# A hybrid decoder layer on one core: the gated linear units ahead of the first two heads' chains, the convolution beside them

## The chip, the core and the metric

The kernel runs on one core of a Trainium2 chip, as one launch. The metric is the device time in microseconds (us). The core has a matrix engine (PE), a vector engine (DVE), an engine for activations and copies (ACT), a general engine (POOL) and an engine that issues DMAs (SP). Each works through its own list of instructions in order and waits for the others by semaphores; the transfers run on DMA queues.

## The reference

One layer for 512 prompt tokens and 8 samples of 8 tokens, 576 columns in all. Shortened:

```
x  = x + 0.5 * swiglu(rmsnorm(x))                       # ffn1, 1024 -> 2816 -> 1024
z  = rmsnorm(x) @ w_in                                  # inputs of all branches and three gates
y_a = rwkv7(z)        # 8 heads of 64: s = s*w + (s@-kk)*kka + v*k per token, o = s@r;
                      # then group norm, + bonus, * g, @ w_rwkv_out
u   = z[:256] * sigmoid(z[256:512])                     # gated linear unit (GLU)
y_b = silu(layernorm(depthwise_conv31(u))) @ w_conv_out # convolution of 31 taps
y_c = cross_attention(z, 256 memory tokens) @ w_xattn_out
m   = sum(sigmoid(gate_n) * y_n for n in a, b, c) @ w_o # merge
x   = x + m
x   = x + 0.5 * swiglu(rmsnorm(x)); y = rmsnorm(x)     # ffn2
```

The new states of the heads, of the token shift and of the convolution are returned too.

## The kernel before

All activations lie with channels on the 128 partitions and the 576 tokens along the free dimension, in two halves of 288 columns. A product in full precision is made of three products of parts: `split` (L94 to L96) rounds an operand to a high part (ACT, L95) and subtracts it for a low part (DVE, L96); L109 multiplies high by high, high by low, low by high. So a projection of 128 rows over 1024 inputs is 48 products of 288 columns on L109, and it needs `wh` from ACT and `wl` from DVE.

The program is ffn1, then the middle, then the merge and ffn2. The middle is written out as a list of steps, `PLAN` (L28), and the instructions of every engine get their place by a scheduler that walks through the program in this order and lets later work in where an earlier one would wait. The steps are:

- A0: the cross-attention, whose result is `oc`.
- P0 to P3, `prep`: the four pairs of heads (128 channels each). Each makes three projections (144 products), the decay factors (a reciprocal, L888), the keys' norm (L137, L147), factors `ra`, `kb`, and the masked products of these, `gr` (PE L945, DVE L947). The last L947 of a pair ends its part that the inverse needs.
- I0 to I3, `inverse`: a triangular inverse by elimination on DVE. A DMA takes the blocks out of `gr` and back into `lt` (L1031, L1033, on SP), then come L1034 to L1049, and DMAs bring the result back.
- J0 to J3, `joined`: 32 small products of PE for it (L1067, L1075), with a copy on ACT between (L1070).
- B0 and B2, `chains`: for two pairs, eight chunks of 64 tokens one after another, each with small products (L1122, L1132, L1139), copies (L1137, L1140), the product for the state (L1143) and the new state on DVE (L1165); then the sample's chunk and `mixed` for both pairs, with the group norm (L984, L137, L147) and DVE's L990, L992, L994, L997.
- G0, `glu`: four projections, 192 products, for the convolution's input.
- C0, `conv`: on DVE, 60 taps of 512 columns (L730) and 60 of 64 columns (L731) with L727 at the start of each half, then the layer norm over channels (PE L127, L137, L147).
- Y, X, Z with a count: the gates of the three branches, eight of each, which nothing before the merge waits for. A Y block is one projection (48 products) and a store; X (after the attention) and Z (after the convolution, whose result is split to `cb0h`) are a projection and 12 products more, a multiplication on DVE (L858), a sum with what is stored already (L862) and a store.
- L0, `load_ya`, and then the merge.

The gates are the work that fills PE while DVE does the inverses and the chains. Step P1's function stands under the same name as P2's, so a line tells the kind of work and not its pair.

Ahead of ffn1, `busy` (L209) gives PE a number of products of zeros while the first inputs are loaded (POOL's memset, L224, releases them). `low_rank`, at the start of the middle, makes decay, learning rate and gate of the heads in products of 288 columns; the gates' eviction from PSUM is L691.

Of the kernel before, what the change touches and what calls it, by code (L numbers as in the profile page):

```python
# [9 lines left out]
ALU = mybir.AluOpType  # L10
# [14 lines left out]
NORMED = 1  # L25

ROOMS = (8, 9, 10, 11, 12, 0, 1, 2, 3, 4, 8, 9, 10, 11, 5, 6, 7, 0, 8, 9, 10, 11)
PLAN = ("A0 P0 I0 Y3 G0 P1 J0 I1 Y3 X1 J1 B0 X3 P2 I2 Y2 X2 P3 J2 X2 I3 C0 Z2 J3 B2 Z4 L0 Z2")  # L28
PADN = 8 * 65 + 8 * 9
GRP = 11  # L30
NPROB = 36
# [18 lines left out]
class _Builder:  # L50
# [122 lines left out]
    def build(self):  # L173
        tc, a = self.tc, self.a
        with ExitStack() as st:
# [22 lines left out]
            with ExitStack() as sf:  # L198
                F = sf.enter_context
                self.psum(F, p=8)  # L200
                x1p = F(tc.tile_pool(name="x1", bufs=1))
                fp = F(tc.tile_pool(name="f1", bufs=2))
                hp = F(tc.tile_pool(name="h1", bufs=1))
                self.strassen_pools(F)
                self.weight_pools(F, 2, 1)
                x = [x1p.tile([128, N], F32, name=f"x{k}") for k in range(8)]
                idle = fp.tile([128, H], F32, name="m1")[:, :128]
                self.G.memset(idle, 0.0)
                self.busy(idle, idle, 16)  # L209
                self.dma(x[0][:, :H], a["x"][:, 0, :H])  # L210
                self.dma(self.pv, a["pv"])
                raw = []
                for k in range(4):
                    w = self.wtile()
                    raw += [w[:, 384 * k:384 * (k + 1)] for k in range(2)]
                for k in range(8):
                    if k:
                        self.dma(x[k], a["x"][:, k, :])
                    self.dma(raw[k].rearrange("p (j c) -> p j c", j=3),
                             a["wu1"][:3, :, 128 * k:128 * (k + 1)].rearrange("j p c -> p j c"))  # L220
                    if not k:
                        self.dma(x[0][:, H:], a["x"][:, 0, H:])
                self.dma(self.cst, a["cst"])
                self.G.memset(self.eps[:, 0:1], 64e-5)  # L224
                self.G.memset(self.eps[:, 1:2], 1e-5)
                self.A.activation(self.eps[:, 0:1], self.eps[:, 0:1], AF.Copy)
                c = _COLS["mu"]
                self.V.tensor_scalar(self.omu, self.pv[:, c:c + 15], -1.0, 1.0, ALU.mult, ALU.add)
                c = _COLS["ka"]
                self.V.tensor_scalar(self.oka, self.pv[:, c:c + 4], -1.0, 1.0, ALU.mult, ALU.add)  # L230
                self.ffn(x, hp, fp, "g1", a["wu1"], a["wd1"], self.mix_norm, raw, lambda: self.mem_load(mp),
                         (self.mem_k, self.mem_v))
# [18 lines left out]
                    "Z": [(lambda i=i: self.gated(gp, 1, "cb", self.cb, i, 0)) for i in range(8)]}  # L251
            for step in PLAN.split():
                n = int(step[1:])
# [377 lines left out]
    def low_rank(self, zp):  # L631

        V, A, T, a, b1 = self.V, self.A, self.T, self.a, self.b1
        two = lambda name, n: zp.tile([128, 2, n], F32R, name=name)
        sub = lambda o, x, hi: V.tensor_tensor(o, x, hi.bitcast(F32), ALU.subtract)
        wh, wl, gh, gl = two("wh", 512), zp.tile([128, 512], F32R, name="wl"), two("gh", 512), zp.tile(
            [128, 512], F32R, name="gl")
        xs, lg, gs = two("xs", N), two("lg", N), zp.tile([128, N], F32R, name="gs")  # L640
        x = b1.tile([128, N], F32, name="k")
        self.shifted(12, x, b1)
        A.activation(x[:64], x[:64], AF.Tanh)
        for i in range(2):
            o, q = slice(64 * i, 64 * i + 64), slice(64 - 64 * i, 128 - 64 * i)
            A.copy(xs[o, i], x[o])
            sub(xs[q, i], x[o], xs[o, i])
        x = b1.tile([128, N], F32, name="r")
        self.shifted(13, x, b1)
        A.activation(x, x, AF.Sigmoid)  # L650
        self.split(lg[:, 0], lg[:, 1], x)
        x = b1.tile([128, N], F32, name="av")[:96]
        self.shifted(14, x, b1)
        A.activation(x, x, AF.Sigmoid)
        A.copy(gs[:96], x)
        sub(gs[32:64], x[32:64], gs[32:64])

        t = b1.tile([128, 1024], F32, name="lt")
        self.dma(t, a["wda"])
        t = t.rearrange("p (i c) -> p i c", i=2)  # L660
        A.copy(wh, t)
        for i in range(2):
            o = slice(64 * i, 64 * i + 64)
            sub(wl[o], t[o, i], wh[o, i])
        t = [b1.tile([128, PADN], F32, name=n)[:, :512] for n in ("w", "g")]
        for i in range(2):
            self.dma(t[i], a["wg"][:, 512 * i:512 * i + 512])
            A.copy(gh[:, i], t[i])
        sub(gl, t[0], gh[:, 0])
        sub(gh[64:96, 1], t[1][64:96], gh[64:96, 1])  # L670

        def products(*ops):
            for h in range(2):
                c = slice(h * H, (h + 1) * H)
                p = self.bank("g")[:, :H]
                for q, (l, r) in enumerate(ops):
                    T.matmul(p, l, r[:, c], start=q == 0, stop=q == len(ops) - 1)  # L677
                yield c, p

        for j in range(4):  # L680
            ch = slice(128 * j, 128 * j + 128)
            for i, (par, out, name) in enumerate((("w0", self.d_w, "bv"), ("a0", self.d_a, ("k", "r")[j % 2]))):
                t = b1.tile([128, N], F32, name=name, bufs=2 - i)
                o = slice(64 * i, 64 * i + 64)
                for c, p in products((wh[:, i, ch], xs[:, i]), (wl[o, ch], xs[o, i])):
                    A.activation(t[:, c], p, AF.Sigmoid, bias=self.par(par, j))
                self.store(out[j], t)
            t = b1.tile([128, N], F32, name=("av", "zt")[j % 2])
            for c, p in products((gh[:, 0, ch], lg[:, 0]), (gh[:, 0, ch], lg[:, 1]), (gl[:, ch], lg[:, 0]),
                                 (gh[:96, 1, ch], gs[:96])):  # L690
                A.copy(t[:, c], p)  # L691
            self.store(self.d_gt[j], t)


# [670 lines left out]
```

## Time and profile before

| | us |
|---|---|
| timed, three runs: median (lowest, highest) | 1507.62 (1499.61, 1508.52) |
| profiled execution, its own time | 1491.07 |
| its span | 1489.2 |
| PE, DVE, ACT busy | 1449.4, 1028.1, 664.4 |
| granted clock of PE, mean | 0.974 |
| middle stage, first rows of A0 to the merge | about 445 to 1001 |

Busy shares are of the span. In the table of stretches that follows in the prediction, an engine's busy time is given with its count of records, and PEclk is the share of its full clock that PE was granted.

### The profile page before, as it was taken

The page shows a single profiled execution, that of the slowest core. Times are in us where ns is not written, and L with a number is a line of the kernel's source. Part 1 is how long each engine was busy: PE and PEld are TensorE (multiplying, and loading weights), DVE is VectorE, ACT ScalarE, POOL GpSimd, SP SyncE. Part 2 cuts the span into 40 slices and gives each one's busy share as a digit, 9 for nine tenths or more (in the row PEclk, how much of TensorE's full clock was granted, in tenths as well). Part 3 has the DMA queues.
Part 4 walks back from the last instruction along what each step waited for, and adds up shares of the span by engine and source line. Part 5 has one row for each costly group of instructions (what it writes and reads, how often), then busy time and mean ns, then how long its engine had stood idle before and what let it go on. Part 6 is the DMA issues. An engine that isn't in the chain of part 4 may idle for free.

```text
span 1489.2 us, 27301 instructions
## 1 busy us (share of the span) xinstructions
PE 1449.4 (97%) x10884; PEld 1384.6 (93%) x10884; DVE 1028.1 (69%) x2059; ACT 664.4 (45%) x1348; POOL 5.0 (0%) x22
## 2 busy tenths in 40 slices
PE   9999999999999999999999887999999999999998
PEld 9999999999988889899889786889999999999997
DVE  7976777777875629896347763348578767777775
ACT  7443444444577733534355422344444433444442
POOL 0000000000000000000000000000000000000000
PEclk9999999999999999999999877989999999999999
DMA  6222222323644143344122332227322322233221
GB/s 209 72 86 86 86 85 86 98 88 99 198 149 154 57 140 80 89 124 117 49 89 88 92 114 75 74 87 258 101 85 72 94 78 86 89 89 107 85 86 64
DMA packets 98444, 151.28 MB, mean 102 GB/s; under 512 B 43997, under 2 KB 53725, under 8 KB 98317
## 3 DMA queue, kind: packets, MB, share of 16 engines
q1 hardware_dynamic: 97740, 148.95, 32.2%
q8 instruction: 85, 1.39, 0.4%
q10 hardware_dynamic: 576, 0.59, 0.1%
q14 instruction: 43, 0.34, 0.1%
HBM read 130.03 MB, written 19.48 MB: 100 GB/s over the span
## 4 chain that ended last, share of the span: by engine, by line
PE 90%; DVE 6%; issue 1%; ACT 1%; DMA 1%; SPq 0%; DVEq 0%; POOL 0%; ACTq 0%; POOLq 0%
PE p L109 50%; PE p L384 26%; DVE pr L1045 2%; DVE tt L1047 1%; PE g L945 1%; DVE wl L96 1%; PE g L677 1%; PE c L1122 1%; PE g L1153 1%; PE c L1139 1%; PE g L137 1%; DVE cc L730 1%; PE c L1086 1%; PE g L147 1%; PE c L1132 1%
## 5 line engine op out<-in xcount | busy, mean ns | idle before, releaser
L109 PE MATMUL p<-x,wh 128*128 128x288 f32 x3136 | 653.7, 301 | 4.2 <-ACT wh L95 3.5
L109 PEld LDWEIGHTS p<-x,wh 128*128 128x128 f32 x3136 | 511.8, 191 | 12.4 <-ACT wh L95 4.2
L109 PE MATMUL p<-x,wl 128*128 128x288 f32 x1568 | 472.0, 302 | 6.8 <-DVE wl L96 6.7
L95 ACT CAST wh<-w 128x512 fp32r<-128x512 f32 (+1 forms) x354 | 210.3, 600 | 260.9 <-PE p L384 100.0
L109 PEld LDWEIGHTS p<-x,wl 128*128 128x128 f32 x1568 | 298.5, 191 | 12.9 <-DVE wl L96 8.7
L96 DVE TENSOR_TENSOR wl<-w,wh 128x512 fp32r<-128x512 f32 (+1 forms) x354 | 232.5, 662 | 109.8 <-ACT wh L95 99.5
L384 PE MATMUL p<-t,wh 128*128 128x288 f32 x1088 | 224.3, 299 | 0.0
L384 PEld LDWEIGHTS p<-t,wh 128*128 128x128 f32 x1088 | 173.9, 188 | 6.4 <-DVE t L395 6.4
L384 PE MATMUL p<-b,wh 128*128 128x288 f32 x816 | 169.7, 295 | 0.0
L384 PE MATMUL p<-t,wl 128*128 128x288 f32 x544 | 160.6, 295 | 0.0
L95 ACT CAST wh<-p 128x512 fp32r<-128x512 f32 x136 | 84.5, 621 | 155.9 <-PE p L109 117.4
L384 PEld LDWEIGHTS p<-b,wh 128*128 128x128 f32 x816 | 132.8, 188 | 0.0
L96 DVE TENSOR_TENSOR wl<-p,wh 128x512 fp32r<-128x512 f32 x136 | 93.6, 688 | 50.6 <-ACT wh L95 47.8
L384 PE MATMUL p<-b,wl 128*128 128x288 f32 x408 | 120.4, 295 | 0.0
L384 PEld LDWEIGHTS p<-t,wl 128*128 128x128 f32 x544 | 102.5, 188 | 0.0
L384 PEld LDWEIGHTS p<-b,wl 128*128 128x128 f32 x408 | 76.8, 188 | 0.0
L462 DVE SCALAR_TENSOR_TENSOR x<-p,x 128x288 f32<-128x288 f32 x128 | 57.8, 451 | 21.2 <-PE p L109 21.2
L95 ACT CAST x<-t 128x576 fp32r<-128x576 f32 (+1 forms) x60 | 36.5, 610 | 44.8 <-DVE t L466 42.2
L374 DVE TENSOR_TENSOR p<-w 128x512 f32<-128x512 f32 x68 | 46.7, 686 | 2.4 <-DMA w<-wu 2.0
L374 DVE TENSOR_TENSOR p<-p,w 128x512 f32<-128x512 f32 x68 | 46.4, 682 | 0.1
L851 ACT ACTIVATE gate<-p 128x288 f32<-128x288 f32 x48 | 19.7, 410 | 55.9 <-PE p L109 50.6
L1165 DVE SCALAR_TENSOR_TENSOR st<-c,gc,mg 64x64 f32<-64x64 f32 x56 | 15.8, 283 | 41.3 <-PE c L1143 28.9
(380 smaller groups left out, 1990.9 us busy)
## 6 DMA issues: line engine op xcount, KB each, us to landing
w<-wu SPq DMA_DIRECT2D x85, 512.0 KB
w<-win SPq DMA_DIRECT2D x44, 512.0 KB
w<-wd SPq DMA_DIRECT2D x64, 256.0 KB
w<-wd SPq DMA_DIRECT2D x16, 384.0 KB
d_mb<-gate SPq DMA_DIRECT2D x16, 288.0 KB
w<-wo SPq DMA_DIRECT2D x8, 512.0 KB
d_x<-x SPq DMA_DIRECT2D x16, 144.0 KB
d_g<-gate SPq DMA_DIRECT2D x8, 288.0 KB
```

The lines of the kernel that those rows point to most:

```text
L95: self.A.copy(hi, x)
L96: self.V.tensor_tensor(lo, x, hi.bitcast(F32), ALU.subtract)
L109: self.T.matmul(p, l, x[r][:, c], start=k == 0 and i == 0, stop=k == n - 1 and i == 2)
L137: self.T.matmul(p[:, i * w:(i + 1) * w], t[:, o:o + 128], sel, start=q == 0, stop=q == len(ops) - 1)
L147: self.T.matmul(p[:, o + f - d.start:o + 128 - d.start], r[f:, i], self.con("ident")[f:, f:], start=True, stop=True)
L374: V.tensor_tensor(s, u, v, ALU.add)
L384: self.T.matmul(p, hl[l][:, c], xs[k][b][:, o], start=first and k == 0 and q == 0, stop=k == 3 and q == 2, skip_group_check=True)
L462: V.scalar_tensor_tensor(x[m][:, c], p, 0.5, x[m][:, c], ALU.mult, ALU.add)
L677: T.matmul(p, l, r[:, c], start=q == 0, stop=q == len(ops) - 1)
L851: self.A.activation(g[:, c], p, AF.Sigmoid)
L1045: V.tensor_tensor(pr, tt[:, :n, :e].unsqueeze(2).broadcast_to([np_, n, m, e]), l3[:, t:e, :e].unsqueeze(1).broadcast_to([np_, n, m, e]), A ...
L1165: V.scalar_tensor_tensor(mn[s, i, s], p, g[s], mg[s, s], ALU.mult, ALU.add)
```

## The change

The list of steps is written anew, the lead has ten empty products in place of 16, and one eviction of `low_rank` goes from ACT to DVE:

```
-PLAN = ("A0 P0 I0 Y3 G0 P1 J0 I1 Y3 X1 J1 B0 X3 P2 I2 Y2 X2 P3 J2 X2 I3 C0 Z2 J3 B2 Z4 L0 Z2")
+PLAN = "A0 P0 I0 Y2 P1 J0 Y3 I1 Y3 X2 J1 X1 G0 B0 C0 P2 I2 X3 P3 J2 X2 Z1 I3 Z2 J3 B2 Z5 L0"
...
-                self.busy(idle, idle, 16)
+                self.busy(idle, idle, 10)
...
             for c, p in products((gh[:, 0, ch], lg[:, 0]), (gh[:, 0, ch], lg[:, 1]), (gl[:, ch], lg[:, 0]),
                                  (gh[:96, 1, ch], gs[:96])):
-                A.copy(t[:, c], p)
+                V.tensor_scalar(t[:, c], p, 1.0, None, ALU.mult)
```

So G0 goes from behind the first Y blocks to the place directly ahead of B0, and C0 from behind I3 to behind B0; all eight Y blocks stand ahead of the first chains.

The first place to look at is PE's list at the end of the first chains, where the mixing (L984, L137, L147) ends. Before (`oc` is the attention's result, so the L109 rows are products of an X block):

```order
L984 MATMUL g<-ra,cst 128x320
L984 MATMUL c<-ra,cst 128x256
L137 MATMUL c<-cst,u_8234 128x2 x2
L984 MATMUL g<-ra,cst 128x256
L109 MATMUL p<-oc1h,wh 128x288
L109 MATMUL p<-oc1l,wh 128x288
L109 MATMUL p<-oc1h,wl 128x288
L109 MATMUL p<-oc0h,wh 128x288
L137 MATMUL c<-cst,u_8234 128x2 x3
L109 MATMUL p<-oc0l,wh 128x288
```

And now (`cc` is the convolution's result, `x` the normed input):

```order
L984 MATMUL g<-ra,cst 128x320
L984 MATMUL c<-ra,cst 128x256
L137 MATMUL c<-cst,u_8528 128x2 x2
L984 MATMUL g<-ra,cst 128x256
L137 MATMUL c<-cst,u_8528 128x2 x3
L147 MATMUL c<-cst,u_8547 128x128 x4
L147 MATMUL c<-cst,u_8547 128x64
L137 MATMUL g<-cst,u_8564 128x2 x5
L147 MATMUL g<-cst,u_8583 128x128 x4
L147 MATMUL g<-cst,u_8583 128x64
L127 MATMUL g<-cc_7900,cst 128x288 x2
L109 MATMUL p<-x_4949,wl 128x288
```

The products of gates and projections between the steps of the mixing are gone from there; directly behind the mixing stand the convolution's first statistic and a product of P2 with a low part of its weight.

The second place is DVE's list at the same point, behind the L992 of the second pair. Before:

```order
L992 TENSOR_TENSOR u_8271<-u_8271,g 128x512
L992 TENSOR_TENSOR u_8271<-u_8271,g 128x64
L96 TENSOR_TENSOR wl<-w,wh 128x512
L858 TENSOR_TENSOR gate<-p,gate 128x288
L994 TENSOR_TENSOR u_8271<-u_8271,bv 128x576
L858 TENSOR_TENSOR gate<-p,gate 128x288
L997 TENSOR_TENSOR u_8271<-gt,u_8271 128x576
L911 TENSOR_SCALAR rt<-rt 128x10
```

And now, the first rows of a longer piece:

```order
L992 TENSOR_TENSOR u_8565<-u_8565,g 128x512
L992 TENSOR_TENSOR u_8565<-u_8565,g 128x64
L730 SCALAR_TENSOR_TENSOR cc_7900<-up_7902,pv,cc_7900 128x512
L730 SCALAR_TENSOR_TENSOR cc_7901<-up_8034,pv,cc_7901 128x512
L994 TENSOR_TENSOR u_8565<-u_8565,bv 128x576
L730 SCALAR_TENSOR_TENSOR cc_7901<-up_8034,pv,cc_7901 128x512
L731 SCALAR_TENSOR_TENSOR cc_7901<-ue_8035,pv,cc_7901 128x64
L997 TENSOR_TENSOR u_8565<-gt,u_8565 128x576
```

Then come seven more pairs of an L730 and an L731, and then the last rows up to the first L96:

```order
L730 SCALAR_TENSOR_TENSOR cc_7901<-up_8034,pv,cc_7901 128x512
L604 SCALAR_TENSOR_TENSOR k<-z_5305,omu,zt 128x512
L730 SCALAR_TENSOR_TENSOR cc_7901<-up_8034,pv,cc_7901 128x512
L605 SCALAR_TENSOR_TENSOR k<-z_5305,omu,zt 128x64
L730 SCALAR_TENSOR_TENSOR cc_7901<-up_8034,pv,cc_7901 128x512
L96 TENSOR_TENSOR wl<-w,wh 128x512
```

So the first weight split behind L992, which came next before, now has 13 L730 and 8 L731 ahead of it; it is the one that the P2 product of the PE piece reads. Nine L730 more come behind it, between splits.

The third place is DVE's list ahead of inverse 3, whose first instruction is the L1034. Before, the last of the convolution's products (L746) and the splits of its result stand there:

```order
L746 TENSOR_TENSOR cc_6823<-cc_6823,g 128x64
L746 TENSOR_TENSOR cc_6824<-cc_6824,g 128x64
L96 TENSOR_TENSOR wl<-w,wh 128x512 x2
L96 TENSOR_TENSOR cb0l<-cc_6823,cb0h 128x576
L96 TENSOR_TENSOR cb1l<-cc_6824,cb1h 128x576
L858 TENSOR_TENSOR gate<-p,gate 128x288 x2
L96 TENSOR_TENSOR wl<-w,wh 128x256
L862 TENSOR_TENSOR gate<-gate,gm 128x576
L858 TENSOR_TENSOR gate<-p,gate 128x288 x2
L1034 MEMSET lt 108x32
```

And now, behind pair 3's last masks:

```order
L947 TENSOR_TENSOR gr<-g,cst 128x128 x2
L858 TENSOR_TENSOR gate<-p,gate 128x288 x2
L96 TENSOR_TENSOR wl<-w,wh 128x512 x2
L96 TENSOR_TENSOR wl<-w,wh 128x256
L96 TENSOR_TENSOR wl<-w,wh 128x512 x2
L858 TENSOR_TENSOR gate<-p,gate 128x288 x2
L96 TENSOR_TENSOR wl<-w,wh 128x256
L96 TENSOR_TENSOR wl<-w,wh 128x512 x2
L858 TENSOR_TENSOR gate<-p,gate 128x288 x2
L862 TENSOR_TENSOR gate<-gate,gm 128x576
L1034 MEMSET lt 108x32
```

The convolution is gone from this piece, and three gates' multiplications (L858) with the splits of their weights stand between the last masks and the inverse; the last pair is that of the Z block which the list of steps has ahead of I3.

## The prediction

> **What bounds the kernel now.** I read the page's shares first, then a table of stretches, then PE's waits.
>
> ```profile
> span 1489.2 us, 27301 instructions
> ...
> PE 1449.4 (97%) x10884; PEld 1384.6 (93%) x10884; DVE 1028.1 (69%) x2059; ACT 664.4 (45%) x1348; POOL 5.0 (0%) x22
> ...
> PEclk9999999999999999999999877989999999999999
> ```
>
> PE is the bound. The time that another order can win is what PE loses: its idle time and its low clock, and the clock row shows that the low clock lies in slices 23 to 27 of 40, some 820 to 1010 us. So I cut the middle at the points where PE goes from one plan step to the next (columns: stretch, its length, busy time of each engine with its count of records, granted clock, DMA).
>
> ```profile
> core 0: us, PE busy (x) PEld busy (x) DVE busy (x) ACT busy (x) POOL busy (x), PEclk, DMA share, GB/s
> 559.00:607.00 48.00, 45.20 (x305) 43.83 (x304) 44.72 (x95) 17.68 (x39) 0.00 (x0) 0.90 0.34 92
> 706.90:801.60 94.70, 94.30 (x788) 81.00 (x788) 47.02 (x100) 41.67 (x110) 0.00 (x0) 0.98 0.24 73
> 801.60:869.10 67.50, 60.29 (x402) 56.60 (x400) 44.60 (x110) 31.84 (x58) 0.00 (x0) 0.90 0.36 100
> 869.10:912.50 43.40, 29.71 (x246) 28.52 (x245) 29.39 (x73) 9.36 (x21) 0.00 (x0) 0.85 0.34 96
> 912.50:1001.10 88.60, 85.73 (x701) 71.94 (x701) 33.92 (x76) 35.83 (x94) 0.00 (x0) 0.84 0.24 69
> 1050.00:1075.00 25.00, 25.00 (x191) 25.00 (x190) 15.15 (x24) 10.18 (x16) 0.00 (x0) 1.00 0.28 95
> 900.00:925.00 25.00, 16.44 (x157) 15.19 (x158) 5.98 (x13) 5.67 (x14) 0.00 (x0) 0.70 0.38 97
> ```
>
> The stretch from 1050 is PE at its best: 25.00 / 191 = **0.131 us for a product** of 288 columns. The five stretches of the argument are: S1, the start to the first state product of the first chains (706.9); S2, from there to the last mask of pair 2 (801.6); S3, to J2 (869.1); S4, J2 to J3 (912.5); S5, J3 to the merge (1001.1). S1 and S2 are dense; S3 and S4 have 7.2 and 13.7 us without PE.
>
> ```profile
> PE p L109 <- DVE wl L96: 6.7, 5, 3.2
> PE c L1067 <- DMA aux<-s: 6.1, 1, 6.1
> PE p L109 <- ACT cb0h L95: 5.4, 1, 5.4
> ```
>
> These waits (from 400 to 1010 us) are for the convolution's result cb0h, for weight splits that stand behind the convolution on DVE, and for inverse 3. A wait costs twice, for the clock of 900 to 925 is 0.70 after the 6.1 us before J3.
>
> **S1.** The new plan lists, ahead of the first chains, eight Y blocks (before: six, and 54 products of the next two), the GLU, P1, and three X blocks (before four), and no P2 (before its 144 projection products). That is 42 - 60 - 144 = -162 products, and 162 x 0.131 = -21.3. Of the loss in 559 to 607 (2.8 idle and a tenth of the clock, 7 in all), where DVE was full at 44.72 of 48.00 beside the GLU, I take back 4.5 of 7, as G0 no longer stands there. Against this J1 now comes too early for inverse 1. What lies between a pair's last mask and its join:
>
> ```profile
> 801.76 1.88 SPq L1031 DMA_DIRECT2D s<-gr  x2
> 815.16 0.09 DVE L1034 MEMSET lt<- 108x32 f32 x1
> 852.01 0.53 DVE L1047 TENSOR_REDUCE tt<-pr 108x11 f32<-108x352 f32 x1
> 869.69 0.09 DVE L1034 MEMSET lt<- 108x32 f32 x1
> 900.96 0.51 DVE L1047 TENSOR_REDUCE tt<-pr 108x11 f32<-108x352 f32 x1
> 869.08 1.19 PE L1067 MATMUL c<-aux,gr 32*32 32x32 f32 x32
> 912.49 1.91 PE L1067 MATMUL c<-aux,gr 32*32 32x32 f32 x32 [6.09 <-DMA aux<-s]
> ```
>
> For pair 2 the way from the mask's store to the first elimination step took 815.16 - 801.76 = 13.4. For pair 3 the elimination took 901.47 - 869.69 = 31.8 and the way back 912.49 - 901.47 = 11.0. Inverse 1 has fewer foreign instructions between its steps than inverse 3, so I take 27, and 4.5 for its load behind a gate's store on SP: 13.4 + 27 + 11.0 + 4.5 = 56. PE has 335 products and some small ones for it, 48.5. So J1 waits 7.5 (bounds 0 and 12.3, by 31.8 in place of 27). S1 = -21.3 - 4.5 + 7.5 = **-18** (bounds -26 and -13).
>
> **S2.** Here the 48 of the 60 long convolution taps that the list of DVE places behind the first state update come in. Of the timeline of before (start, length), the ends of the parts of S2, two vector instructions of it, and the convolution's statistics on PE:
>
> ```profile
> 706.90 0.45 PE L1143 MATMUL c<-vu,kbt 128*64 128x64 f32 x8
> 774.83 0.43 PE L147 MATMUL g<-cst,u 64*128 64x64 f32 x2
> 776.22 1.17 PE L137 MATMUL g<-cst,u 128*128 128x2 f32 x10
> 801.36 0.29 DVE L947 TENSOR_TENSOR gr<-g,cst 128x128 f32<-128x128 f32 x1
> 776.69 0.76 DVE L994 TENSOR_TENSOR u<-u,bv 128x576 f32<-128x576 f32 x1
> 803.92 0.28 DVE L605 SCALAR_TENSOR_TENSOR r<-z,omu,zt 128x64 f32<-128x64 f32 x1
> 834.37 2.10 PE L127 MATMUL g<-cc,cst 128*128 128x288 f32 x8
> 849.01 1.41 PE L147 MATMUL g<-cst,rt 128*128 128x128 f32 x10
> ```
>
> The convolution's taps, all of them in one group each (busy us, mean ns):
>
> ```profile
> L730 DVE SCALAR_TENSOR_TENSOR cc<-up,pv,cc 128x512 f32<-128x512 f32 x60 | 43.3, 743 | 0.0
> L731 DVE SCALAR_TENSOR_TENSOR cc<-ue,pv,cc 128x64 f32<-128x64 f32 x60 | 14.3, 279 | 0.2
> ```
>
> And PE's products of L109 alone (PE, PEld) beside the chains:
>
> ```profile
> 707.00:775.30 68.30, 27.93 (x157) 21.96 (x158) 0.98 0.21 62
> ```
>
> The chains took 775.26 - 706.90 = 68.4, with 157 products of fill beside them. Now the fill is 54 products of P2, and none in the last four chunks and in the mixing behind them. If every product that goes shortens the chains they take 68.4 - 103 x 0.131 = 54.9; if the chains bind themselves, 68.4. PE was busy 94.30 of 94.70, so the nearer end is the lower: I take a third of the way, **59.5**. Then PE stands. P2's next product reads a weight's low half (L96), and the list of DVE has 13 L730, 8 L731, L994, L997, L604 and L605 ahead of it: 13 x 0.72 (43.3 / 60) + 8 x 0.24 (14.3 / 60) + 2 x 0.76 + 0.76 (L604, taken as L994) + 0.28 + 0.7 (L96, estimated by L994 too) = 14.5 from the end of the last L992, which is over about when PE is. Behind the product that waits, all of PE's list waits: P2's projections, the statistics, masks and X blocks. With a little of the 14.5 done beside the mixing I take **13** (bounds 0, if DVE is that far by then, and 15). Behind it are 87 products, 11.4, with the convolution's statistics among them; in S3 before, these took 849.01 - 834.37 = 14.6 with fill beside them, and DVE's last nine taps (6.5, with splits between them) end behind the first 50 products (6.6), so that the second of the statistics may wait. I take 11.4 + 7.6 = **19** (bounds 12 and 26). From pair 2's own L137 to its last mask took 801.65 - 776.22 = 25.4; I take **28**, since the stores and splits queued from the wait must be worked off first (bounds 25.4 and 31). Sum 59.5 + 13 + 19 + 28 = 119.5 against 94.7: **+25** (bounds -2 and +46).
>
> **S3.** The convolution leaves the stretch, and pair 3's projections and X blocks stay beside inverse 2, at 13.4 + 37.3 (852.54 - 815.16, the elimination with what stands between) + 11.0 + 5 for a load behind a store = 66.7 for 67.5, and the last part of P3 stands behind inverse 2 on DVE (its mask work on PE waits for L928 there, some 2 us). I take **+1** (bounds -8 and +6).
>
> **S4.** Inverse 3's first step stands on DVE behind Z's multiplication (L858), whose products follow J2 on PE: 97 products (37 of X, 60 of Z), 12.7, and their small waits and the store ahead of the load on SP, 6.3. 19 + 31.8 + 11.0 = 62 against 43.4: **+18.6**. Without that PE's own work would set it: 379 products x 0.131 = 49.6 and 5 of J2 and masks, 54.7, or +11.3, and that is the lower bound; the upper is +24, with 5 for a clock as after the wait before J3.
>
> **S5** has 48 products fewer beside the chains: **-6.3** (0 to -13, as the clock there was 0.84 and may be nearer to 1). Merge to end is the same list.
>
> **The lead and the evictions.**
>
> ```profile
> 0.99 5.95 PE L170 MATMUL p<-m 128*128 128x128 f32 x32 [0.99 <-POOL eps L224]
> 6.70 5.54 PE L109 MATMUL p<-x,t 128*128 128x288 f32 x40
> ```
>
> ```profile
> L691 ACT COPY zt<-g 128x288 f32<-128x288 f32 x4 | 1.6, 395 | 0.2
> L858 DVE TENSOR_TENSOR gate<-p,gate 128x288 f32<-128x288 f32 x32 | 14.6, 455 | 20.6 <-ACT gate L851 10.4 <-PE p L109 9.6 <-ACT vu L1140 0.6
> ```
>
> The 16 empty products leave 32 records, 5.95 / 32 = 0.186 each, so ten (20 records) end near 4.7. The first real product could start about 5.0 instead of 6.70: -1.7 (bounds -1.9, and +1.7 if its operands come no sooner and run at a lower clock). The Trainium skill ("TensorE: Matmul & The Clock Gate", Part 1, on the warm-up) says that the clock doubles after a window of about 3.4 us of busy time which runs free of the kernel's start, and counts no products; by it 3.7 us of empty products may end inside a window, real products then run at half clock for up to another 3.4 us, and this term is 0 in place of -1.7 (an estimate), the sum +20.3. No run here shows a lead of 3.7 us; behind the 5.95 of this one, 40 real products took 5.54, 0.139 each, nearly the full pace.
>
> Eight evictions of 288 columns go from ACT (0.395) to DVE, 3.2 less there and, by L858 of the same size, 8 x 0.455 = 3.6 more here. They lie under the wide projections of the attention's stretch, before 559 us; the work that hides them is PE's, so 0 (bounds -1.6 and +3.6).
>
> **Sum:** -18 + 25 + 1 + 18.6 - 6.3 - 1.7 = **+18.6**. The profiled execution took 1491.07, its span 1489.2, and would take 1509.7; the timed runs' median is 1507.62, 16.6 above it, so the forecast is 1526.
>
> **Rivals.**
>
> *The convolution fits into the chains' gaps (faster, about 1486, 0.22).* DVE was busy 47.02 of S2's 94.70; the 48 long and 8 short taps make 34.7 + 1.9, so 83.6: there is room. If DVE is through with them when the mixing ends, S2 = 54.9 + 0 + 11.4 + 2 + 25.4 = 93.7, -1; inverse 1 with 1 us of wait gives S1 -24.8, S4 +11.3. The sum is -24.8 - 1 + 1 + 11.3 - 6.3 - 1.7 = -21.5. The point is S2 below about 100: from there on the whole is faster by over 1%. Against it: PE has no fill in the last four chunks, so the chains' end is early and DVE has less time, not 94.7.
>
> *It cancels (within 1%, about 1511, 0.28).* Half of the wait, 6.5, and inverse 3 not held up, S4 +12: S2 then 110, and the sum -18 + 15 + 1 + 12 - 6.3 - 1.7 = +2, or +4 with J1 waiting 2 more. It speaks for it that each of my waits can only be smaller if PE is late.
>
> *The clock falls as well (slower, about 1545, 0.04).* Three new waits of 7 to 13 us (J1, P2, J3) each bring what 900 to 925 shows, 0.30 of 25 = 7.5 us. 18.6 + 2.5 x 7.5 = +37. The Trainium skill ("TensorE: Matmul & The Clock Gate", Part 1, the two states) says that an idle window of about 3.4 us halves the clock and a busy one of that length restores it; by it, an estimate, each wait costs 1.7 more, 5 in all, and the sum would be +24. The row shows more, as 25 us were held at 0.70.
>
> The forecast with +12 to +28 has 0.46.
>
> **Chances and range.** 1% (15 us) is about what a measurement of this kernel can tell from none. Faster by over 1%: 0.22; within: 0.28; slower: 0.50. The forecast's own range is 1519 to 1536. For 8 in 10 the range goes down to 1484, through the cancelling case and to the middle of the fast one, and up to 1548, with the upper part of S2's bounds and most of the slow clock.
>
> **What would show it.** In the changed kernel: PE waits for J1 about 7 us at the join's L1067; a wait of about 13 on DVE wl L96 after the last L147 of the first chains; L730 rows between L1165 rows; the last mask of pair 2 about 120 after the first L1143; inverse 3's L1034 19 us after J2 and a wait of about 7 before J3; no wait for cb0h. I am wrong if DVE has the taps done by the mixing's end, or if the chains with less fill take 68 again and the wait vanishes in that.

## The result, and the profile after

The changed kernel took **1522.24 us** (median of four runs, 1517.52 to 1526.69), the kernel before 1506.66 (four runs, 1499.61 to 1508.52). The ratio is 1.0112, with a 95% interval of 1.0062 to 1.0161, so 15.6 us slower; the forecast was 1526, or 18 us. In a later comparison of the same two kernels the ratio was 1.0168 (1.0095 to 1.0240). The page of the changed kernel's profiled execution, the lines that answer to those of before:

```profile
span 1515.7 us, 27281 instructions
...
PE 1465.2 (97%) x10872; PEld 1398.6 (92%) x10872; DVE 1038.8 (69%) x2067; ACT 657.7 (43%) x1337; POOL 5.0 (0%) x22
...
PEclk9999999999999999999579899799999999999999
```

The span is 26.5 us longer than that of before (1489.2). It is more than the 15.6 of the medians, since the profiled execution of before, 1491.07, lay below all of its first four timed runs, while that of the changed kernel is its fastest. The shares of the engines say nothing of it; the clock row does: its lowest digits, a 5 and a 7, now stand in slices 20 and 21, at 720 to 796, where before stood nines; another 7 stands in slice 26, in the second chains.

The stretches, cut at the same steps (the first state product, pair 2's last mask, J2, J3, the merge), and ahead of them the one from 559 on:

```profile
core 0: us, PE busy (x) PEld busy (x) DVE busy (x) ACT busy (x) POOL busy (x), PEclk, DMA share, GB/s
559.00:607.00 48.00, 45.61 (x363) 42.76 (x363) 30.63 (x57) 24.93 (x57) 0.00 (x0) 0.93 0.38 97
685.80:817.60 131.80, 111.26 (x789) 94.37 (x789) 87.54 (x170) 49.59 (x123) 0.00 (x0) 0.79 0.17 45
720.00:757.50 37.50, 31.46 (x174) 25.81 (x174) 20.40 (x38) 11.64 (x33) 0.00 (x0) 0.59 0.09 19
817.60:883.30 65.70, 60.96 (x400) 56.48 (x399) 41.38 (x101) 25.55 (x55) 0.00 (x0) 0.87 0.29 78
883.30:940.00 56.70, 54.48 (x451) 53.40 (x450) 36.39 (x87) 17.20 (x38) 0.00 (x0) 1.00 0.49 146
940.00:1024.00 84.00, 78.42 (x652) 65.20 (x652) 34.68 (x76) 34.45 (x91) 0.00 (x0) 0.85 0.31 91
1024.00:1515.70 491.70, 483.65 (x3594) 479.72 (x3594) 351.24 (x652) 197.69 (x352) 0.00 (x0) 0.99 0.31 97
```

| | before | changed | difference | forecast |
|---|---|---|---|---|
| S1 with the lead | 706.9 | 685.8 | -21.1 | -19.7 |
| S2 | 94.7 | 131.8 | +37.1 | +25 |
| S3 | 67.5 | 65.7 | -1.8 | +1 |
| S4 | 43.4 | 56.7 | +13.3 | +18.6 |
| S5 | 88.6 | 84.0 | -4.6 | -6.3 |
| merge to end | 488.1 | 491.7 | +3.6 | 0 |

S2 is the whole of the loss and more. Its row says what is wrong in it: 20.5 us without PE, and a clock of 0.79. S4 is the opposite, 54.48 of 56.70 busy at a clock of 1.00, where before had 13.7 idle. The waits of PE that ended last on DVE or on a DMA, from 440 to 1030 (total, times, longest):

```profile
PE p L109 <- DVE wl L96: 16.5, 5, 10.0
PE g L127 <- DVE k L928: 3.9, 1, 3.9
PE c L1067 <- DMA aux<-s: 0.8, 1, 0.8
```

The 10.0 is the wait behind the first chains. In the timeline of PE (start, length, then idle time ahead and what ended it) it stands right behind the mixing:

```profile
754.81 2.69 PE L147 MATMUL g<-cst,u 128*128 128x128 f32 x10 [1.73 <-ACT u L154]
758.57 2.26 PE L127 MATMUL g<-cc,cst 128*128 128x288 f32 x4 [1.07 <-DVE cc L730]
770.79 0.61 PE L109 MATMUL p<-x,wl 128*128 128x288 f32 x1 [9.96 <-DVE wl L96]
```

And in that of DVE the split that ends it comes behind the last of the taps that the list has ahead of it:

```profile
769.40 0.74 DVE L730 SCALAR_TENSOR_TENSOR cc<-up,pv,cc 128x512 f32<-128x512 f32 x1
770.06 0.68 DVE L96 TENSOR_TENSOR wl<-w,wh 128x512 fp32r<-128x512 f32 x1
```

### The profile page after: what moved, and what is told of

It is laid out like the page before. It is cut to its first block, busy times and chain, and to the rows that moved or that the text cites. A ratio compares the mean times of both kernels' runs of the same rounds, so it can differ in the third digit from the quotient of the medians.

```text
span 1515.7 us, 27281 instructions
## 1 busy us (share of the span) xinstructions
PE 1465.2 (97%) x10872; PEld 1398.6 (92%) x10872; DVE 1038.8 (69%) x2067; ACT 657.7 (43%) x1337; POOL 5.0 (0%) x22
## 5 line engine op out<-in xcount | busy, mean ns | idle before, releaser
L109 PE MATMUL p<-x,wh 128*128 128x288 f32 x3136 | 651.5, 300 | 3.1 <-ACT wh L95 1.2
L109 PEld LDWEIGHTS p<-x,wh 128*128 128x128 f32 x3136 | 511.2, 190 | 11.8 <-issue 3.4
L109 PE MATMUL p<-x,wl 128*128 128x288 f32 x1568 | 470.7, 301 | 14.9 <-DVE wl L96 14.6
L96 DVE TENSOR_TENSOR wl<-w,wh 128x512 fp32r<-128x512 f32 (+1 forms) x354 | 232.2, 662 | 147.7 <-ACT wh L95 136.7
L109 PEld LDWEIGHTS p<-x,wl 128*128 128x128 f32 x1568 | 297.8, 190 | 21.7 <-DVE wl L96 17.1
L95 ACT CAST wh<-p 128x512 fp32r<-128x512 f32 x136 | 84.5, 621 | 156.4 <-PE p L109 117.3
L96 DVE TENSOR_TENSOR wl<-p,wh 128x512 fp32r<-128x512 f32 x136 | 93.6, 688 | 51.1 <-ACT wh L95 48.2
L374 DVE TENSOR_TENSOR p<-w 128x512 f32<-128x512 f32 x68 | 46.6, 686 | 2.2 <-DMA w<-wu 1.6
L1045 DVE TENSOR_TENSOR pr<-tt,lt 108x6 f32<-108x6 f32 (+9 forms) x80 | 42.4, 530 | 1.9
L730 DVE SCALAR_TENSOR_TENSOR cc<-up,pv,cc 128x512 f32<-128x512 f32 x60 | 43.3, 743 | 0.4
```

The costliest lines, as they stand in the source:

```text
L95: self.A.copy(hi, x)
L96: self.V.tensor_tensor(lo, x, hi.bitcast(F32), ALU.subtract)
L109: self.T.matmul(p, l, x[r][:, c], start=k == 0 and i == 0, stop=k == n - 1 and i == 2)
L374: V.tensor_tensor(s, u, v, ALU.add)
L730: V.scalar_tensor_tensor(c[:, :SEQ], up[:, k:k + SEQ], w, c[:, :SEQ], ALU.mult, ALU.add)
L1045: V.tensor_tensor(pr, tt[:, :n, :e].unsqueeze(2).broadcast_to([np_, n, m, e]), l3[:, t:e, :e].unsqueeze(1).broadcast_to([np_, n, m, e]), A ...
```

## The experiments

Two theories were on trial at first. The one: the taps that now stand ahead of pair 2's weight splits on DVE cost the time, as they hold P2 and so leave PE without fill. The other: the gates and projections, moved as such, cost it. From the third experiment on the clock was the question, and then the GLU's place. The chains below are the stretch from the first state product to the end of the last L147 of their mixing.

**1. The small parts alone.** The list of steps of before, with the rest of the change.

```
-PLAN = "A0 P0 I0 Y2 P1 J0 Y3 I1 Y3 X2 J1 X1 G0 B0 C0 P2 I2 X3 P3 J2 X2 Z1 I3 Z2 J3 B2 Z5 L0"
+PLAN = ("A0 P0 I0 Y3 G0 P1 J0 I1 Y3 X1 J1 B0 X3 P2 I2 Y2 X2 P3 J2 X2 I3 C0 Z2 J3 B2 Z4 L0 Z2")
```

> The list of steps of before, with the ten empty products and the evictions of L691 on DVE. Theory (the loss is the new list's, the small parts hide or gain): the first real product starts at 5.3 instead of 6.7, the evictions show nowhere, so -1.4 and, within what can be measured, no change to before (0.99 to 1.005). Rival (the evictions on DVE, 3.6 us, or a lead too short for the clock cost time): +2 to +5, a lower clock in the first 25 us, and the merge later than 1001 by that.

Measured: 0.9965 of before (0.9919 to 1.0012). As expected; the loss is the list's.

**2. X3 ahead of the convolution.**

```
-... G0 B0 C0 P2 I2 X3 P3 ...
+... G0 B0 X3 C0 P2 I2 P3 ...
```

> The changed kernel with X3 ahead of the convolution in the list (G0 B0 X3 C0 P2 I2 P3). Theory (the first chains ran at half clock and 71.7 long because PE had no fill in their second half): the fill is back, the granted clock in the chains is 0.95 or more, they take 66 to 70, the 10 us wait for the weight split is gone, and S2 (131.8) becomes about 120 though it holds 180 products (23.6 us) more; S3 then lacks these and stays at 64 to 68 by inverse 2, with over 15 us of idle PE. In all about -10, a span of 1500 to 1511. Rival (the taps between the state updates on DVE slow the chains, with fill or without): chains of 72 or more, S2 140 or more, a span of 1520 or more.

Measured: 1.0094 (1.0061 to 1.0126), a span of 1520.8. Its S2, cut where the mixing ends:

```profile
691.30:768.30 77.00, 76.20 (x622) 63.42 (x621) 43.58 (x92) 32.36 (x86) 0.00 (x0) 0.91 0.24 65
768.30:833.90 65.60, 55.01 (x367) 50.62 (x367) 51.42 (x94) 30.26 (x65) 0.00 (x0) 0.90 0.19 62
```

The clock of the chains is higher (0.91 for 0.78), with the fill, but S2 is 142.6: P2 still stands behind the taps, and a wait of 6.8 us for its weight split is left. The total was a miss: fill alone gives nothing back, if P2 comes no sooner. All three numbers of the rival came true (chains of 77.0, S2 of 142.6, a span of 1520.8), but its reason doesn't follow from that: in experiments 7 and 8 the chains took 78.9 without a tap beside them and 78.7 with 31 long ones.

**3. The convolution behind P2.**

```
-... G0 B0 C0 P2 I2 X3 P3 ...
+... G0 B0 P2 C0 I2 X3 P3 ...
```

> The changed kernel with the convolution one step later in the list (G0 B0 P2 C0 I2 X3 P3). Theory (where the taps stand against pair 2's weight splits sets the loss, and not the GLU and gates ahead of the chains): pair 2's products become the chains' fill, their clock is 0.95 or more, pair 2's last mask comes 95 to 108 after the first state product instead of 131.8, and S3 stays within 62 to 72; in all -20 to -30, a span of 1486 to 1496, which is before or a little better. Rival (S2 is long because the gates no longer stand beside the chains, wherever the taps are): S2 120 or more, or what S2 wins S3 loses (80 or more) since the taps then hold inverse 2; a span of 1508 or more.

Measured: 1.0096 (1.0044 to 1.0147), a span of 1517.7. Pair 2's last mask came 99.4 after the first state product, and S3 took 67.3, both as expected; the clock of 0.95 was not, since P2's products fill only the first part of S2 (the first row below is the rest of it, at 0.58). The 32 us were given back later all the same:

```profile
744.60:786.50 41.90, 27.96 (x133) 23.94 (x129) 34.13 (x68) 13.12 (x30) 0.00 (x0) 0.58 0.17 51
853.80:920.90 67.10, 65.55 (x530) 62.48 (x529) 42.02 (x98) 21.81 (x48) 0.00 (x0) 1.00 0.44 128
920.90:975.00 54.10, 53.00 (x395) 43.86 (x394) 16.39 (x39) 15.45 (x48) 0.00 (x0) 0.65 0.22 65
975.00:1026.90 51.90, 47.65 (x321) 40.21 (x319) 20.25 (x43) 22.29 (x50) 0.00 (x0) 0.80 0.23 67
```

S4 (the second row) is now 67.1 long and full of gates' products, which is more than inverse 3 needs; the second chains (the last two rows) are 106.0 for 84.0, at clocks of 0.65 and 0.80, though PE is busy in 53.00 of the first 54.10. So a clock may be low where PE has no gap worth the name. The second chains hold 64 records more here than in the changed kernel. The first kernel of experiment 7, which takes as long as before, has nearly the same (its S4 and S5):

```profile
864.30:910.90 46.60, 39.48 (x306) 38.34 (x305) 31.65 (x77) 12.04 (x27) 0.00 (x0) 0.85 0.49 141
910.90:1016.70 105.80, 100.60 (x713) 84.09 (x713) 35.99 (x80) 37.26 (x96) 0.00 (x0) 0.73 0.22 63
```

So beside that kernel the loss is in S4, 67.1 for 46.6: it holds 224 records more, and S2, at 659 records in place of 868, holds 209 fewer. Work that does not fill S2 comes back in S4.

**4. Seven taps of 31.**

```
-            for k in range(31):
+            for k in range(7):
```

> The changed kernel with 7 of the convolution's 31 taps, so 24 are left out in each half: 48 L730 (35 us of DVE) and 48 L731 less, most of which stood beside the first chains. Theory (the taps ahead of the weight splits on DVE make the wait and the missing fill): no wait over 2 us for a weight split between the chains and pair 2's mask, clock 0.95 or more in the chains; S2 and S3 together shorter by 20 to 35 than the changed kernel's 197.5, a span of 1481 to 1496. Rival (the new order of gates sets the loss): the two together shorter by less than 10, a span of 1506 or more.

Measured, one execution: a span of 1504.8, between the two. S2 (119.8) and S3 (59.4) are 18.3 shorter than in the changed kernel, with no wait over 1.3 us for a split, and the chains are full of P2's products; S5 is 15.8 longer, at a clock of 0.77. The 20 to 35 and the clock of 0.95 were missed (the chains took 80.7, at 0.83). So the taps make the wait and keep P2 out of the chains, but taking them away shortens S2 by only 12.0 of the 37.1 that it grew, and S2 then holds 872 records for 789. S5 stays open: the changed kernel itself took 84.0 there in its first execution and 94.3 in its second (experiment 9), so one execution can't settle it.

**5. Unread products of 128 columns in the chains.** Into columns of a chunk's bank that nothing uses:

```
+    def hold(self, ps, n):
+        l = self.xn[0][0]
+        for _ in range(n):
+            self.T.matmul(ps[:, 384:512], l[:, :128], l[:, :128], start=True, stop=True, skip_group_check=True)
...
+            self.hold(ps, 8)     # three times in each of the first chains' chunks 4 to 7
...
+            self.hold(q, 12)     # behind each L984 of their mixing
```

> The changed kernel with 144 more products of 128x128, whose result nobody reads, in the last four chunks of the first chains and in their mixing; nothing else moves up to there. Theory (the clock falls where PE's products are few and small for some 7 us, even if it has no gap): the granted clock of 720 to 757, 0.59 in the changed kernel, is 0.9 or more, and the way from the first state product to the last L147 of the mixing is shorter than its 71.7 in spite of the added work: 60 to 68; S2 becomes 118 to 127 for 131.8, the span 1502 to 1511. Rival (the chains bind by their own waits, the low clock goes with these): the added products only lengthen them, 75 or more, a clock under 0.75, a span of 1518 or more.

Measured: 1.0228 (1.0172 to 1.0283). The stretch that they fill, whole (columns as above):

```profile
718.50:793.60 75.10, 72.62 (x382) 64.33 (x381) 40.42 (x79) 14.72 (x40) 0.00 (x0) 0.55 0.09 23
```

And the unread products in it alone (PE, PEld, clock, DMA):

```profile
718.50:793.60 75.10, 32.09 (x133) 28.80 (x132) 0.55 0.09 23
```

PE is busy in 72.62 of 75.10 and its clock is 0.55: the products only lengthen the chains, to 105.1 for 71.7, as the rival has it. Its reason, that the low clock goes with the chains' own waits, does not hold here, since PE hardly waits. The same in the second chains of experiment 1's kernel:

> The list of steps of before, with the two small parts, and 120 and 48 unread products of 128x128 in the second chains, in chunks 0 to 2, 6 and 7 and the mixing, where that kernel had 37 us of busy PE at half clock. Theory (as above): a clock of 0.92 or more from J3 to the merge for 0.77, that stretch 76 to 83 for 87.9, a span of 1474 to 1484 for 1488.9, and 0.984 to 0.993 of the time of before. Rival (the clock follows the waits, the products only add): the stretch 92 or more, the span 1493 or more.

Measured: 1.0095 (1.0048 to 1.0143), for 0.9965 without the products, a miss too.

**6. Unread products of 288 columns instead.** 72 of them, into the free part of the outputs' bank:

```
-            self.hold(ps, 8)     # three times in each chunk
+            self.hold(py[:, 128:128 + H], 4)     # three times in each chunk
```

> As the run with 144 unread products of 128 columns, but with 72 of 288 or 256 columns in the place of these, in the same chunks and mixing of the changed kernel. Theory (the clock goes by how much the array does in some 7 us; a product of 128 columns, which took 0.2 us and more, is too thin, one of 288 in 0.131 us holds the clock as fill does): a granted clock of 0.85 or more in 720 to 757 for 0.59, the way from the first state product to the last L147 of the mixing 60 to 69 for 71.7, the span 1502 to 1513. Rival (no unread product helps, the clock goes by the chains' own waits): a clock under 0.7, 75 or more, a span of 1520 or more.

Measured: 1.0154 (1.0092 to 1.0217), a span of 1511.8. Three stretches of the chains, whole:

```profile
718.20:730.70 12.50, 12.02 (x110) 9.90 (x107) 6.04 (x12) 3.08 (x11) 0.00 (x0) 1.00 0.00 1
730.70:744.40 13.70, 13.52 (x62) 9.23 (x62) 5.95 (x11) 2.54 (x9) 0.00 (x0) 0.50 0.16 30
744.40:758.00 13.60, 11.25 (x94) 10.02 (x94) 10.16 (x19) 5.80 (x16) 0.00 (x0) 1.00 0.07 14
```

And the unread products in them alone:

```profile
718.20:730.70 12.50, 3.58 (x16) 2.39 (x16) 1.00 0.00 1
730.70:744.40 13.70, 4.31 (x12) 3.09 (x12) 0.50 0.16 30
744.40:758.00 13.60, 5.10 (x32) 4.31 (x32) 1.00 0.07 14
```

In the first and the third, with 16 and 32 wide products, the clock is 1.00; in the second, with 12, it is 0.50, and there PE has the least idle time of the three. Over 722.0 to 762.2 it is 0.78, for 0.59 in 720.0 to 757.5 of the changed kernel. That fits the theory's account of the clock, that wide products hold it where there are enough of them. It is not shown by it: the three stretches are cut where the clock changed, a low clock itself makes products rarer, and the second also holds four products each of 320 and of 512 columns. The expected clock of 0.85 was missed, and so was the time, since the products cost more than they win: the way to the last L147 took 75.1 for 71.7. In the second chains likewise:

> The list of steps of before with the two small parts, and 60 and 24 unread products of 288 and 256 columns in the second chains, in chunks 0 to 2, 6 and 7 and the mixing. Theory (as above): a clock of 0.9 or more from J3 to the merge for 0.77, that stretch 77 to 85 for 87.9, 0.985 to 0.995 of the time of before. Rival: the stretch 92 or more, 1.0 or more.

Measured: 1.0066 (1.0028 to 1.0103), for 0.9965 without them: no gain.

**7. The GLU earlier in the changed list.**

```
-A0 P0 I0 Y2 P1 J0 Y3 I1 Y3 X2 J1 X1 G0 B0 C0 ...
+A0 P0 I0 Y2 G0 P1 J0 Y3 I1 Y3 X2 J1 X1 B0 C0 ...
```

> The changed kernel with the GLU back behind the first Y blocks (Y2 G0 P1), all other steps as changed. The taps then run beside inverses 0 and 1, as before, and P2 is the first chains' fill. Theory (the late GLU brings the taps between the chains and P2, and that costs the 10 us wait and the missing fill): no wait over 3 us for a weight split before pair 2's mask, chains of 64 to 70 at a clock of 0.85 or more, S2 105 to 122 for 131.8, and J1 2 to 8 later; a span of 1497 to 1509. Rival (it is the gates: where they stand is what counts, and the GLU's place is indifferent): a span of 1511 or more.

Measured: 1.0019 (0.9978 to 1.0060), a span of 1507.1, and no loss is left that can be told from none. S2:

```profile
687.50:766.40 78.90, 78.90 (x603) 65.90 (x602) 28.81 (x67) 32.52 (x95) 0.00 (x0) 0.84 0.17 46
687.50:805.20 117.70, 115.67 (x868) 100.00 (x868) 51.77 (x116) 57.16 (x135) 0.00 (x0) 0.89 0.21 61
```

P2 fills the chains, PE has no idle time in them, and S2 is 14.1 us shorter, with 79 records more in it. The chains themselves took 78.9, not the 64 to 70 expected: their clock is 0.84, where the kernel before, with nearly as many records (598), had 0.98 and took 68.4 in its one profiled execution; the section on the prediction comes back to this. A second place for it (J0 Y3 G0 I1) does the same:

> The changed kernel with the GLU behind the second Y blocks (J0 Y3 G0 I1), so that the taps run beside inverse 1 and the X blocks, later than with the GLU behind the first Y blocks. Theory (any place from which the taps are through before the chains' second half gives the changed kernel's loss back): P2 fills the chains, no wait over 3 us for a weight split before pair 2's mask, a span of 1495 to 1509, 0.992 to 1.005 of before. Rival (the taps then hold inverse 1 or the chains): J1 or the first state product 8 us or more later than 685.8 without a gain behind it, a span of 1512 or more.

Measured: 1.0016 (0.9985 to 1.0046), a span of 1491.0.

**8. The GLU late, alone.** The list of steps of before, with nothing moved but the GLU.

```
-A0 P0 I0 Y3 G0 P1 J0 I1 Y3 X1 J1 B0 X3 P2 ...
+A0 P0 I0 Y3 P1 J0 I1 Y3 X1 J1 G0 B0 X3 P2 ...
```

> The list of steps of before with the two small parts, and the GLU alone moved, directly ahead of B0 as in the changed kernel; X3 and P2 stand ahead of the convolution here, so the chains keep their fill and the taps stand behind pair 2's splits. Theory A (the late GLU costs by the taps alone, wherever they then stand, since DVE has no idle time left for them beside dense PE work): 1.006 to 1.015 of before. Theory B (what costs is the taps ahead of pair 2's splits, which take the fill off the chains; with the fill kept the late GLU costs little): chains of 66 to 72 at a clock of 0.9 or more, no wait over 3 us for a weight split before pair 2's mask, 0.995 to 1.006 of before.

Measured: 1.0007 (0.9964 to 1.0049), a span of 1491.2: theory B, on the time. Its S2, and of it the part up to the mixing's last L147:

```profile
657.40:736.10 78.70, 78.70 (x607) 64.97 (x606) 39.19 (x84) 29.90 (x84) 0.00 (x0) 0.85 0.22 58
657.40:774.70 117.30, 117.30 (x887) 101.44 (x886) 74.82 (x150) 50.03 (x126) 0.00 (x0) 0.90 0.26 74
```

PE has no idle time in S2 and no wait over 1.4 us for a split, as B has it; the chains are 78.7 long at a clock of 0.85, which is neither's. 31 of the 60 long taps ran in this S2, and PE lost no time there by waiting for them. So the late GLU is not the cause by itself, nor are taps beside the chains. What experiments 7 and 8 leave is the two together that the changed list has: the GLU directly ahead of B0, and the convolution ahead of P2 and X3, so that the taps come between the chains and what would fill them. The wait alone is not the whole of it: in experiment 3 the convolution stands behind P2, though still ahead of X3, and the loss is as large.

**9. The changed kernel again**, on the same chip as experiment 8.

> The changed kernel once more, beside the run before on the same chip, as a measure for the others. If its first time holds: 1.006 to 1.016 of before, with the low clock of the first chains and the wait of about 10 us for a weight split behind them in the profile again. If these came from that one execution: a clock of 0.9 or more in the first chains, or no such wait.

Measured: 1.0168 (1.0095 to 1.0240). The second half of its first chains, and its S2:

```profile
722.00:760.10 38.10, 32.89 (x188) 26.38 (x182) 21.36 (x42) 11.64 (x33) 0.00 (x0) 0.60 0.09 20
688.90:820.50 131.60, 112.04 (x789) 94.32 (x789) 87.59 (x170) 49.45 (x123) 0.00 (x0) 0.79 0.16 45
```

S2's length is within 0.2 us of the first execution's and both clocks within 0.01, and the wait of 10.0 us for a split is there again. The chains took 71.2, for 71.7. The ratio is a little above the 1.006 to 1.016 expected. No version that was tried is faster than the kernel before beyond its interval; the nearest is experiment 1's.

## Why the prediction was right, and where not

**The place and most of the mechanism** were right: the time is lost in S2, PE has no fill in the first chains' second half, and then it waits for a weight split behind 13 long and 8 short taps. By parts of S2, forecast and measured: chains 59.5 and 71.7 (685.8 to 757.5), the wait with the convolution's first statistic 13 and 13.3 (to 770.8), P2's products 19 and 18.2 (to pair 2's L137 at 788.96), to the last mask 28 and 28.6. Undoing it (experiment 7) gives 1.0019 and 1.0016 for 1.0112.

**The step that failed** is in the chains: "If every product that goes shortens the chains they take 68.4 - 103 x 0.131 = 54.9; if the chains bind themselves, 68.4", and a third of the way between. The 103 products went and the chains took 71.7 and, in experiment 9, 71.2, outside both bounds. I had taken PE's busy time for its work at the full clock. The row of 720.0 to 757.5 shows 31.46 of 37.5 busy, at a clock of 0.59 and without one product of 288 columns. The sum had no term for a clock that falls in the chains themselves. The chains' term is short by 12.2 us, of the 12.3 that S2 as a whole is longer than forecast (131.8 for 119.5). The rival in which the clock falls as well had the effect, but put it behind new waits at J1, P2 and J3, of which only P2's came, and not into the chains.

Whether the fill would have kept the clock is less sure than the 68.4 makes it look. The list of before up to there, and so nearly the same chains with fill, was profiled again in experiment 1 and in experiment 6's second kernel, whose unread products come only later. These chains, before first, and then a piece of the last:

```profile
706.90:775.26 68.36, 68.31 (x598) 56.82 (x597) 25.80 (x62) 28.72 (x83) 0.00 (x0) 0.98 0.21 61
697.60:770.90 73.30, 73.30 (x611) 61.84 (x610) 26.57 (x63) 31.03 (x84) 0.00 (x0) 0.92 0.19 53
700.30:784.80 84.50, 84.50 (x611) 70.51 (x610) 26.57 (x63) 31.13 (x84) 0.00 (x0) 0.79 0.17 47
750.00:770.00 20.00, 20.00 (x90) 14.88 (x91) 5.32 (x13) 4.95 (x17) 0.00 (x0) 0.51 0.16 30
```

Though they differ by only 13 records, the chains took from 68.4 to 84.5 us, and their clock can halve for 20 us although fill stands there and the profile has PE busy throughout. So the chains without fill are 3.3 longer than the shortest of the three and shorter than the other two. That they fell to 0.59 and 0.60 in both executions for want of fill fits experiment 2, but was not shown. What stands is S2 as a whole: 94.7, 99.9 and 111.1 in these three, 131.8 and 131.6 in the changed kernel.

**Smaller misses.** J1's wait of 7.5 was 0: inverse 1's elimination took 25.9 for 27 and the load stood less far behind the store, so the way from mask to join was 50.7 for 56, and PE was at work all that time. S4: inverse 3 began 16.9 us after J2 (forecast 19) and J3 waited 0.8 (forecast about 7); S4 came out near its lower bound, PE's own work, 56.7 for 54.7. From the merge on, +3.6 was not forecast: the mixing's last L147 had waited 3.07 us, and the products behind it began at a low clock, 55 records in the first 10 us at 0.71 for 76 at 1.00 before, which is 21 x 0.131 = 2.8 us. The lead gave 1.4 of 1.7, and the half clock that the prediction allows for behind it did not come (1.00 from 5 to 10 us):

```profile
0.99 4.63 PE L170 MATMUL p<-m 128*128 128x128 f32 x20 [0.99 <-POOL eps L224]
5.27 9.00 PE L109 MATMUL p<-x,t 128*128 128x288 f32 x61
```

The errors have both signs, -1.4 in S1, +12.1 in S2, -2.8 in S3, -5.3 in S4, +1.7 in S5 and +3.6 behind, 7.9 in all on the profiled executions; that the median came within 4 us of the forecast is partly luck, since the profiled execution of before, from which the rows of the sum were taken, was a quick one.

**A misreading** that did not enter the sum: I wrote that in the kernel before the weight splits of S3 and S4 stand behind the convolution, and that it leaves these stretches. That is true of its layer norm, not of its taps. Of DVE's L730 alone, before:

```profile
560.00:607.00 47.00, 15.30 (x21) 0.91 0.34 91
607.00:650.00 43.00, 16.73 (x24) 1.00 0.33 96
650.00:707.00 57.00, 11.30 (x15) 1.00 0.41 116
```

All 60 long taps were done there before the first chains, beside inverse 1 and under PE's gates; only the layer norm behind them stood at C0 in the list. The plan's place of C0 is not the taps' time: the scheduler pulls them up to where the GLU lets them start. That is why moving the GLU behind inverse 1 moved the taps by some 100 us, and it would have been the first thing to look up.

**The fast rival** fell with its premise. DVE did have room (20.40 busy of 37.5 in 720.0 to 757.5), but the room is waits of its own list: L1165, L990 and L992 stand between the taps and wait for PE and ACT, and no tap passes them.

## What to carry to other kernels

Work taken from beside a chain of small products need not shorten the chain: here the granted clock was 0.59 and 0.60 where none was left, and the chain took 71.7 us where the count of products promised 59.5. So price such a move by a stretch of the trace that has no fill, with its clock, and by more than one execution, since the same chains with fill took 68.4, 73.3 and 84.5. When a table moves a step, look up in the trace when its instructions really ran before; its place in the list does not tell (the taps ran long before theirs). And a gain in one stretch (experiment 3 won 32 us in S2) is no gain until the stretches are added up to which the work has moved.

## What the runs showed of the hardware

The granted clock does not go by gaps alone. Of 75.10 us in experiment 5, PE was busy in 72.62 and had 0.55 of its clock, with 133 products of 128 columns among its work; in experiment 6, 16 and 32 unread products of 288 or 256 columns in 12.50 and 13.60 us went with 1.00, and 12 in 13.70 with 0.50; in that experiment's second kernel, 15 products of 288 columns in 20.00 us of the first chains went with 0.51, PE busy throughout. The Trainium skill ("TensorE: Matmul & The Clock Gate", Part 1, the two states) has the clock halved after an idle window of about 3.4 us; these rows agree with the two levels, and by that rule a window must be able to count as idle in which the profile has PE busy nearly throughout. Why the products of 128 columns did not hold the clock wasn't settled: whether by their columns or by how much of the time the array is really at work. One was about as long as a wide one: at full clock, the first eight of experiment 5 took 1.11 us, 0.139 each, against 0.131 for one of 288 columns.
